# Attention encoder on one core: norm and table work moved between VectorE, ScalarE and GpSimd, inverse sums by transposed columns, value bank copied whole

## The chip, the cores and the metric

The kernel runs on one core of a Trainium2 chip. A core has a matrix engine (TensorE, PE), three engines for elementwise work (VectorE or DVE, ScalarE or ACT, GpSimd or POOL), a queue that issues transfers (SyncE, SP), a working memory (SBUF) and a small accumulator memory (PSUM), of which this kernel uses eight banks of 128 partitions by 512 fp32 columns. Each engine works through its own list of instructions in order and waits on semaphores for the others. The metric is the device time of one execution in microseconds.

## The reference

A layer over 2048 tokens of width 1024, one batch, all in fp32. The rows of x are normalised, scaled and shifted by functions of c, and projected by one matrix whose columns belong to three groups of heads. Each head's output is multiplied by a SiLU gate, all are concatenated, projected, gated, added to x, and normalised once more.

```python
h = rmsnorm(x, norm_g) * (1.0 + scale[:, None, :]) + shift[:, None, :]
z = h @ w_in                        # queries, keys, values, gates of A, B, C
a_out = mla_mixer(...)              # 6 heads, low-rank q and kv, block-causal
b_out = chunk_band_mixer(...)       # 5 heads, own chunk + 8 before, relative bias
c_out = forgetting_mixer(...)       # 5 heads, causal, cumulated forget logits
y = concatenate([a_out * silu(a_gate), b_out * silu(b_gate),
                 c_out * silu(c_gate)], axis=-1) @ w_out
x = x + gate[:, None, :] * y
return rmsnorm(x, final_g)
# each head: p = softmax(where(mask, s, NEG)); out = p @ v
```

## The kernel before

The tokens are done in two halves of 1024. In each half a projection stage (`stage_lv`) makes the latents, the values and the rotated queries and keys and stores them to DRAM. Then `attention` goes over 16 heads, two blocks of 512 queries each. To keep fp32 accuracy with the fast matmul type (fp32r), operands are split into a high part, rounded by an ACT copy, and a low part, the difference, and products are made of two or three matmuls.

A block of a head goes over tiles of 128 keys. For each tile PE makes scores in a PSUM bank `st` (three of these), ACT takes three exponentials of it (L753 the high part `ph`, L754 the sum's term `p`, L756 back into PSUM), DVE subtracts to get the low part `pl` (L762), POOL adds up `p` (L767), and PE multiplies `ph` and `pl` with the values into the one bank `pv` (L776, L777). At a block's end `end` (L779) copies `pv` in two pieces and POOL adds and gates them. Then come three steps at fixed distances of tiles, 1, 3 and 5: `sums` (L790) transposes the accumulated terms and reduces them, `rows` (L801) transposes the four inverse sums into rows and splits them, and `gate` (L808) spreads the rows over the partitions with a selecting matmul and multiplies. The maxima of the next block (`max_units`, L950 and L1036) and their transposition into a query row (`m_rows`) run beside this. All of these use two PSUM banks `mx`.

Projections of later heads, the gates, and for the second half the normalised and turned x (`h_units`, with bank `pj`) are cut into units and spread over a head's tiles by `Spread`; `mids` says which head carries what. In the first half the gate row is made in head 3, the row norms of the second half's x in head 7, its turned x in heads 14 and 15. In the second half `out_units` (output projection, residual, final norm) for eight of the 16 row tiles runs in heads 14 and 15, the other eight after them.

The Tile framework orders each engine's instructions from this program when it is built; the order is fixed then. It also keeps two engines from using one PSUM bank at the same time, so a bank passes from engine to engine with a wait.

Of the kernel before, what the change touches and what calls it, by code (L numbers as in the profile page):

```python
# [61 lines left out]
def kernel(ctx: ExitStack, tc: tile.TileContext, a: dict, out: bass.AP):  # L62
# [109 lines left out]
    def x_norm(xt, sq, r):  # L172
# [3 lines left out]
        V.tensor_scalar(vv, ss, 1.0 / D, EPS, op0=ALU.mult, op1=ALU.add)  # L176
        rsqrt(vv, 1, "xr", r)

    def h_units(hT, x_of, xn_of, tmp_of, ptag, norms=None):

        pairs = []
        for p2 in range(4):
            xns = []

            def norm(j, p2=p2, xns=xns):
# [7 lines left out]
                V.tensor_scalar(xn, xt, r, 0.0, op0=ALU.mult, op1=ALU.add)  # L193
                xns.append(xn)

            def turn(k, p2=p2, xns=xns, box={}):
# [10 lines left out]
                V.tensor_copy(hi, tmp)  # L207
# [153 lines left out]
    counters = {"m": 0, "r": 0, "p": 0}  # L361
# [74 lines left out]
    def latents(half, hT, wt, wt_pool, pool, lath, latl, h_pairs):  # L436
# [266 lines left out]
    def m_rows(pool, box, pm_of, dst, c8=None):  # L703
# [22 lines left out]
    def body_units(pool, kind, tb, par, scale, qk, V_of, sg_of, dst):  # L726
# [605 lines left out]
```

## Time and profile before

| | us |
|---|---|
| three runs | 1878.16, 1883.21, 1881.51 |
| median | 1881.51 |
| profiled execution | 1887.48 |
| its span, first to last instruction | 1885.4 |
| PE busy | 1743.9 |
| DVE busy | 1254.3 |
| ACT busy | 1181.6 |
| POOL busy | 985.7 |

Busy time is the time in which at least one instruction of the engine runs. Matmuls are pipelined: one of 512 columns is shown with about 0.40 us while the next starts about 0.23 us after it, so short waits of PE are hidden inside its busy time. The granted clock of PE over the whole run is 0.979.

The run falls into these parts: the start up to about 37 us, the first half's projections to about 250 us, its attention to about 755 us, the second half's projections to about 950 us, its attention to about 1790 us, and the last eight row tiles of the output.

### The profile page before, as it was taken

What the parts mean: (1) busy time and instruction counts of PE and PEld (TensorE: products, weight loads), DVE (VectorE), ACT (ScalarE), POOL (GpSimd) and SP (SyncE); (2) the same over time, 40 slices, a digit from 0 to 9 for tenths busy, and PEclk for the clock granted to TensorE, in tenths of its full rate; (3) what the DMA queues carried; (4) which work ended last, traced back from release to release, by engine and by line L of the source; (5) the groups of instructions that cost most, each with busy time, mean ns of one, the idle gap of its engine ahead of it and who ended that gap; (6) DMA issues with size and microseconds to landing.
All of it is one profiled execution on the core that took longest, in us unless ns stands there. A gap on an engine that the chain in (4) does not pass through costs nothing.

```text
span 1885.4 us, 28584 instructions
## 1 busy us (share of the span) xinstructions
PE 1743.9 (92%) x8899; PEld 1429.7 (76%) x8899; DVE 1254.3 (67%) x2905; ACT 1181.6 (63%) x2614; POOL 985.7 (52%) x902
## 2 busy tenths in 40 slices
PE   2999989998999997999999999999999989899897
PEld 2899877777777775999778777777777767677786
DVE  7663557777667679454466667787788887666543
ACT  2552357577667777342456677899899888555511
POOL 0320146555455557120145555677777788566744
PEclk9999999999999999999999999999999999999999
DMA  7524836335223232144933232222333344232243
GB/s 267 171 76 135 243 110 177 97 107 167 70 75 103 83 115 68 57 131 119 253 101 96 72 91 68 71 71 67 96 99 87 87 137 131 65 101 71 70 137 112
DMA packets 139996, 209.85 MB, mean 111 GB/s; under 512 B 18734, under 2 KB 72494, under 8 KB 139764
## 3 DMA queue, kind: packets, MB, share of 16 engines
q1 hardware_dynamic: 139844, 208.03, 37.2%
q8 instruction: 71, 1.16, 0.3%
q14 instruction: 81, 0.66, 0.1%
HBM read 154.05 MB, written 57.38 MB: 112 GB/s over the span
## 4 chain that ended last, share of the span: by engine, by line
PE 36%; DVE 5%; ACT 5%; issue 3%; POOL 1%; DMA 1%; DVEq 0%; POOLq 0%; ACTq 0%
PE pj L352 5%; PE pj L354 5%; PE pj L353 5%; PE pv L777 3%; PE pv L776 3%; PE st L996 2%; PE st L986 2%; PE mx L1044 2%; PE st L1054 2%; PE st L1055 1%; PE mx L963 1%; PE st L1056 1%; ACT st L756 1%; ACT p L754 1%; DVE pl L762 1%
## 5 line engine op out<-in xcount | busy, mean ns | idle before, releaser
L767 POOL TENSOR_TENSOR p<-p,p 128x512 f32<-128x512 f32 (+3 forms) x516 | 547.5, 1061 | 301.0 <-ACT p L754 267.3
L753 ACT ACTIVATE ph<-st 128x512 fp32r<-128x512 f32 (+1 forms) x580 | 297.7, 513 | 265.4 <-PE st L996 137.5
L762 DVE TENSOR_TENSOR pl<-st,ph 128x512 fp32r<-128x512 f32 (+1 forms) x580 | 333.3, 577 | 175.1 <-ACT st L756 161.2
L756 ACT ACTIVATE st<-st 128x512 f32<-128x512 f32 (+1 forms) x580 | 302.8, 522 | 0.0
L754 ACT ACTIVATE p<-st 128x512 f32<-128x512 f32 (+1 forms) x580 | 296.6, 511 | 0.0
L352 PE MATMUL pj<-hT,whi 128*128 128x512 f32 x544 | 225.3, 414 | 8.5 <-ACT q L920 8.4
L776 PE MATMUL pv<-ph,v 128*128 128x512 f32 (+1 forms) x580 | 215.1, 371 | 11.9 <-ACT ob L784 10.6
L777 PE MATMUL pv<-pl,v 128*128 128x512 f32 (+1 forms) x580 | 213.0, 368 | 12.0 <-DVE pl L762 11.4
L354 PE MATMUL pj<-hT,wlo 128*128 128x512 f32 x544 | 218.6, 402 | 0.0
L353 PE MATMUL pj<-hT,whi 128*128 128x512 f32 x544 | 218.5, 402 | 0.0
L1045 DVE TENSOR_REDUCE pm<-mx 128x1 f32<-128x512 f32 (+2 forms) x240 | 139.5, 603 | 22.6 <-PE mx L1044 20.6
L776 PEld LDWEIGHTS pv<-ph,v 128*128 128x128 f32 x580 | 111.6, 192 | 40.4 <-ACT ob L784 23.1
L777 PEld LDWEIGHTS pv<-pl,v 128*128 128x128 f32 x580 | 111.2, 192 | 38.9 <-DVE pl L762 22.0
L966 DVE TENSOR_REDUCE pm<-mx 128x1 f32<-128x512 f32 (+2 forms) x200 | 116.6, 605 | 30.6 <-PE mx L963 17.1
L996 PE MATMUL st<-q,k 128*128 128x512 f32 (+1 forms) x340 | 124.6, 370 | 0.9 <-DVE q L721 0.7
L785 POOL TENSOR_TENSOR oa<-oa,ob 64x512 f32<-64x512 f32 x64 | 83.7, 1308 | 76.3 <-ACT ob L784 49.8
L352 PEld LDWEIGHTS pj<-hT,whi 128*128 128x128 f32 x544 | 105.0, 193 | 23.8 <-ACT q L920 10.1
L986 PE MATMUL st<-q,k 128*128 128x512 f32 (+1 forms) x340 | 120.8, 356 | 1.2 <-DVE pl L762 0.9
L354 PEld LDWEIGHTS pj<-hT,wlo 128*128 128x128 f32 x544 | 104.4, 192 | 22.1
L353 PEld LDWEIGHTS pj<-hT,whi 128*128 128x128 f32 x544 | 104.8, 193 | 15.9
L1044 PE MATMUL mx<-k,q 128*128 128x512 f32 (+2 forms) x240 | 89.8, 394 | 20.6 <-DVE pm L1045 17.3
L354 PE MATMUL pj<-wo,ol 128*128 128x512 f32 x256 | 102.6, 401 | 2.1 <-POOL ol L1081 2.1
(398 smaller groups left out, 4245.2 us busy)
## 6 DMA issues: line engine op xcount, KB each, us to landing
wr<-in_w_in SPq DMA_DIRECT2D x54, 512.0 KB
wr<-in_x SPq DMA_DIRECT2D x34, 512.0 KB
v<-dva SPq DMA_DIRECT2D x36, 256.0 KB
q<-dqa SPq DMA_DIRECT2D x48, 192.0 KB
k<-dka SPq DMA_DIRECT2D x72, 128.0 KB
wa<-in_w_ada SPq DMA_DIRECT2D x16, 512.0 KB
do<-oo SPq DMA_DIRECT2D x64, 128.0 KB
wr<-do SPq DMA_DIRECT2D x128, 64.0 KB
```

Of the source, the lines that this page charges most:

```text
L352: T.matmul(dst, lhsT=lh, rhs=rh, start=i == 0, stop=False)
L353: T.matmul(dst, lhsT=lh, rhs=rl, start=False, stop=False)
L354: T.matmul(dst, lhsT=ll, rhs=rh, start=False, stop=i == n - 1)
L753: A.activation(ph[:, v0:v1], st[:, v0:v1], AF.Exp, scale=scale)
L754: A.activation(p32[:, v0:v1], st[:, v0:v1], AF.Exp, scale=scale)
L756: A.activation(st[:, v0:v1], st[:, v0:v1], AF.Exp, scale=scale)
L762: V.tensor_tensor(pl[:, c0:c1], st[:, c0:c1], ph[:, c0:c1].bitcast(F32), op=ALU.subtract)
L767: G.tensor_tensor(acc[:, c0:c1], acc[:, c0:c1], p32[:, c0:c1], op=ALU.add)
L776: T.matmul(pv[:, c0:c1], lhsT=vt, rhs=ph[:, c0:c1], start=n == 0, stop=False)
L777: T.matmul(pv[:, c0:c1], lhsT=vt, rhs=pl[:, c0:c1], start=False, stop=n == len(js) - 1)
L986: T.matmul(st[:, c0:c1], lhsT=k2[:, ks], rhs=q2[:, c0:c1], start=True, stop=False)
L996: T.matmul(st[:, c0:c1], lhsT=k1[:, ks], rhs=q1[:, c0:c1], start=False, stop=True)
```

## The change

Row norms: the steps on one number per row go from DVE to POOL. In `h_units` the product with the row norm goes from DVE to ACT, and the high part is made by DVE from PSUM instead of by a cast of ACT's copy. The inverse sums lose the step `rows`; `gate` transposes each column of four, broadcast to 128 columns, and runs three tiles after the block's end instead of five. `end` copies `pv` whole and takes the second copy from SBUF. The gate row is done in eight parts of two halves. The B heads' maxima no longer carry the constant c8 apart; it is taken out of the tables, which POOL scales. `evac` copies the key's high part to `k1` before it makes the low parts. For the eight row tiles of the output that lie in attention, the final norm's scaling is done by ACT and its product with `final_g` by POOL. The second half's turned x lies in heads 13, 14 and 15, and gate projection GA2 in head 12 instead of 13.

```diff
     def rsqrt(v, n, nm, r=None):
         G.tensor_tensor(y, v, mhalf[:, 0:n], op=ALU.pow)
-        V.tensor_tensor(t, y, y, op=ALU.mult)
-        V.tensor_tensor(t, t, v, op=ALU.mult)
-        V.tensor_scalar(t, t, -0.5, 1.5, op0=ALU.mult, op1=ALU.add)
-        V.tensor_tensor(r, y, t, op=ALU.mult)
+        G.tensor_tensor(t, y, y, op=ALU.mult)
+        G.tensor_tensor(t, t, v, op=ALU.mult)
+        G.tensor_scalar(t, t, -0.5, 1.5, op0=ALU.mult, op1=ALU.add)
+        G.tensor_tensor(r, y, t, op=ALU.mult)
...
     def h_units(hT, x_of, xn_of, tmp_of, ptag, norms=None):
-                V.tensor_scalar(xn, xt, r, 0.0, op0=ALU.mult, op1=ALU.add)
+                A.activation(xn, xt, AF.Copy, scale=r)
...
                 A.activation(tmp, tp, AF.Identity, scale=sc1[:, k:k + 1], bias=shf[:, k:k + 1])
-                V.tensor_copy(hi, tmp)
+                V.tensor_scalar(hi, tp, sc1[:, k:k + 1], shf[:, k:k + 1], op0=ALU.mult, op1=ALU.add)
...
     def gate_row(pool):
+        def part(k):
...
+            for c in range(2):
+                sl = slice(512 * c, 512 * c + 512)
+                if k == 0:
+                    V.tensor_scalar(acc[:, sl], wa[:, sl], cact[:, 0:1], 0.0, op0=ALU.mult, op1=ALU.add)
+                else:
+                    V.scalar_tensor_tensor(acc[:, sl], in0=wa[:, sl], scalar=cact[:, k:k + 1], in1=acc[:, sl], op0=ALU.mult, op1=ALU.add)
+        return [lambda k=k: part(k) for k in range(8)] + [lambda: gate_sum(pool, box["acc"])]
...
         def negate():
-            if c8 is None:
-                V.tensor_reduce(mp[:, 96:100], pm_of(), axis=AX.X, op=ALU.max, negate=True)
-            else:
-                m4 = pool.tile([128, 4], F32, tag="m4", name="m4")
-                V.reduce_max(m4, pm_of(), axis=AX.X)
-                V.tensor_scalar(mp[:, 96:100], m4, -1.0, c8(), op0=ALU.mult, op1=ALU.add)
+            V.tensor_reduce(mp[:, 96:100], pm_of(), axis=AX.X, op=ALU.max, negate=True)
...
         def end():
             pv = box["pv"]
+            ob = pool.tile([128, 512], F32, tag="oo", name="ob", bufs=2)
+            A.activation(ob, pv, AF.Copy)
             oa = pool.tile([128, 512], F32, tag="oa", name="oa", bufs=2)
-            A.activation(oa[o0:o1, :], pv[i0:i1, :], AF.Copy)
-            ob = pool.tile([128, 512], F32, tag="oo", name="ob", bufs=2)
-            A.activation(ob[o0:o1, :], pv[o0:o1, :], AF.Copy)
+            A.activation(oa[o0:o1, :], ob[i0:i1, :], AF.Copy)
...
-            rp = box["rp"] = rpads[counters["r"] % 2]
-            V.reciprocal(rp[:, 0:4], s4)
-        def rows():
-            rw = box["rw"] = rrows[counters["r"] % 2]
-            tp = pst("mx")
-            T.transpose(tp[:, 0:128], box["rp"], ident)
-            A.activation(rw[0:64, :], tp[0:64, 0:128], AF.Copy)
-            V.tensor_tensor(rw[64:128, :], tp[0:64, 0:128], rw[0:64, :].bitcast(F32), op=ALU.subtract)
+            rs = box["rs"] = pool.tile([128, 4], F32, tag="rs", name="rs")
+            V.reciprocal(rs, s4)
         def gate():
             rb = pst("mx")
             for t in range(4):
-                T.matmul(rb[:, 128 * t:128 * t + 128], lhsT=sel[:, t, :], rhs=box["rw"], start=True, stop=True)
+                T.transpose(rb[:, 128 * t:128 * t + 128], box["rs"][:, t:t + 1].to_broadcast([128, 128]), ident)
...
     def bias(self):
-            G.tensor_scalar(tb32[:, 0:384], tb32[:, 0:384], c8, 0.0, op0=ALU.add, op1=ALU.add)
-            V.tensor_scalar(tb32[:, 384:640], tb32[:, 384:640], 8.0, 0.0, op0=ALU.mult, op1=ALU.add)
-            V.tensor_scalar(te, te, 8.0, c8, op0=ALU.mult, op1=ALU.subtract)
+            G.tensor_scalar(tb32[:, 384:640], tb32[:, 384:640], 8.0, c8, op0=ALU.mult, op1=ALU.subtract)
+            G.tensor_scalar(te, te, 8.0, c8, op0=ALU.mult, op1=ALU.subtract)
-            evac_split(teh[:, 0:256], tel[:, 0:256], te)
+            A.activation(teh[:, 0:256], te, AF.Copy)
+            G.tensor_tensor(tel[:, 0:256], te, teh[:, 0:256].bitcast(F32), op=ALU.subtract)
...
     def evac(self, b, p):
             A.activation(q1[0:64, :], p[0:64, :], AF.Copy)
-            A.activation(k2[64:128, :], p[64:128, :], AF.Copy)
+            A.activation(k1[0:64, :], p[64:128, :], AF.Copy)
...
-            A.activation(k1[0:64, :], p[64:128, :], AF.Copy)
+            A.activation(k2[64:128, :], p[64:128, :], AF.Copy)
...
     def out_units(pool, wo, gate, fg, i):
             r = rsqrt(vv, 1, "xr")
+            if i < 8:
+                A.activation(xt, xt, AF.Copy, scale=r)
             for c in range(2):
-                V.scalar_tensor_tensor(xt[:, sl], in0=xt[:, sl], scalar=r, in1=fg[c], op0=ALU.mult, op1=ALU.mult)
+                if i < 8:
+                    G.tensor_tensor(xt[:, sl], xt[:, sl], fg[c], op=ALU.mult)
+                else:
+                    V.scalar_tensor_tensor(xt[:, sl], in0=xt[:, sl], scalar=r, in1=fg[c], op0=ALU.mult, op1=ALU.mult)
...
-                    tail.extend((clock[0] + d, u) for d, u in zip((1, 3, 5), t))
+                    tail.extend((clock[0] + d, u) for d, u in zip((1, 3), t))
...
-                mid = {1: "GA0", 2: "G1", 5: "GA1", 6: "G2", 9: "G3", 11: "G4", 13: "GA2"}
+                mid = {1: "GA0", 2: "G1", 5: "GA1", 6: "G2", 9: "G3", 11: "G4", 12: "GA2"}
...
-                mids[3] = mids.get(3, []) + [lambda: gate_row(pool)]
+                mids[3] = mids.get(3, []) + gate_row(pool)
...
-                mids[14] = h1[0] + h1[1]
-                mids[15] = h1[2] + h1[3]
+                h1 = sum(h1, [])
+                mids[13], mids[14], mids[15] = h1[:16], h1[16:32], h1[32:]
```

The order of instructions shows the moves at three places. The first is PE in the last heads of the first half, from the inverse sums of a block to their spreading; `rpad` holds the four inverse sums, `rrow` their rows, `c_ident` is the identity. Before:

```order
L804 MATMUL mx<-c_ident,rpad_253 128x128
L202 MATMUL pj<-c_ident,xn 128x128
L1044 MATMUL mx<-k_8124,q_8133 128x512
L202 MATMUL pj<-c_ident,xn 128x128 x3
L777 MATMUL pv<-pl,v 128x512
L1054 MATMUL st<-q_7821,k_7789 128x128
L1055 MATMUL st<-q_7821,k_7788 128x128
L1056 MATMUL st<-q_7822,k_7788 128x128
L776 MATMUL pv<-ph,v 128x384
L202 MATMUL pj<-c_ident,xn 128x128 x2
L720 MATMUL mx<-c_ident,mpad_251 128x128
L811 MATMUL mx<-rrow_256,sel 128x128 x3
```

After, from the sums of a block (L797) on; `rs` holds the inverse sums:

```order
L797 MATMUL mx<-c_ident,p_7880 128x128 x4
L779 MATMUL pv<-pl,v 128x256
L1050 MATMUL st<-q_7779,k_7733 128x512
L1051 MATMUL st<-q_7779,k_7732 128x512
L202 MATMUL pj<-c_ident,xn 128x128
L778 MATMUL pv<-ph,v 128x128
L1052 MATMUL st<-q_7780,k_7732 128x512 x2
L202 MATMUL pj<-c_ident,xn 128x128 x2
L806 MATMUL mx<-c_ident,rs 128x128 x4
L779 MATMUL pv<-pl,v 128x128
```

The transpose of `rpad` is gone, and the four transposes of `rs` follow the sums' own transposes after seven rows. The line numbers of the changed kernel are its own.

The second is DVE in the same heads, where the second half's x is made; `hT` is the turned x, `htmp` ACT's copy, `xn` the normalised rows. Before:

```order
L207 CAST hT<-htmp 128x256 x2
L721 TENSOR_TENSOR q_8171<-mx,sel 32x512
L796 TENSOR_REDUCE s_8651<-mx 128x4
L208 TENSOR_TENSOR hT<-htmp,hT 128x256
L799 RECIPROCAL rpad_254<-s_8651 128x4
L762 TENSOR_TENSOR pl<-st,ph 128x128
L207 CAST hT<-htmp 128x256 x2
L208 TENSOR_TENSOR hT<-htmp,hT 128x256
L762 TENSOR_TENSOR pl<-st,ph 128x512
L193 TENSOR_SCALAR xn<-wr,norms 128x1024 x2
L806 TENSOR_TENSOR rrow_255<-mx,rrow_255 64x128
```

After:

```order
L718 TENSOR_REDUCE mpad_252<-pm 128x4
L764 TENSOR_TENSOR pl<-st,ph 128x256
L207 TENSOR_SCALAR hT<-pj,sc_72,shf 128x256
L723 TENSOR_TENSOR q_7780<-mx,sel 32x512
L798 TENSOR_REDUCE s_8234<-mx 128x4
L207 TENSOR_SCALAR hT<-pj,sc_72,shf 128x256
L800 RECIPROCAL rs<-s_8234 128x4
L764 TENSOR_TENSOR pl<-st,ph 128x128
L208 TENSOR_TENSOR hT<-htmp,hT 128x256
L764 TENSOR_TENSOR pl<-st,ph 128x512
L207 TENSOR_SCALAR hT<-pj,sc_72,shf 128x256
L808 TENSOR_TENSOR oo<-mx,oa 64x512
```

The product `xn` and the difference `rrow` have left DVE, the casts of `htmp` have become scaled reads of the bank `pj`, and these lie farther apart.

The third is the final norm of the first row tile, before on DVE (`xvv` the mean square, `xrr` the inverse root, `wr` the row tile, `row` a row of `final_g`):

```order
L762 TENSOR_TENSOR pl<-st,ph 128x512
L1102 TENSOR_SCALAR xvv<-xss 128x1
L813 TENSOR_TENSOR oo<-mx,oa 64x512
L152 TENSOR_TENSOR xrt<-xry 128x1
L153 TENSOR_TENSOR xrt<-xrt,xvv 128x1
L154 TENSOR_SCALAR xrt<-xrt 128x1
L156 TENSOR_TENSOR xrr<-xry,xrt 128x1
L1106 SCALAR_TENSOR_TENSOR wr<-wr,xrr,row 128x512 x2
L1045 TENSOR_REDUCE pm<-mx 128x1
```

After, on POOL:

```order
L1092 TENSOR_TENSOR wr<-y,wr 128x512
L1098 TENSOR_SCALAR xvv<-xss 128x1
L150 TENSOR_TENSOR xry<-xvv,mhalf 128x1
L152 TENSOR_TENSOR xrt<-xry 128x1
L153 TENSOR_TENSOR xrt<-xrt,xvv 128x1
L154 TENSOR_SCALAR xrt<-xrt 128x1
L156 TENSOR_TENSOR xrr<-xry,xrt 128x1
L769 TENSOR_TENSOR p_18920<-p_18920,p_19226 128x512
L1105 TENSOR_TENSOR wr<-wr,row 128x512 x2
L1077 TENSOR_TENSOR ol<-wr,oh 128x1024
```

The whole chain and both products stand on POOL now, between additions of `p`; ACT's scaling between them stands on ACT.

## Rows read from the trace of the kernel before

**Rows 1.** The page, part 1: busy us, share of the span, instructions.

```profile
PE 1743.9 (92%) x8899; PEld 1429.7 (76%) x8899; DVE 1254.3 (67%) x2905; ACT 1181.6 (63%) x2614; POOL 985.7 (52%) x902
```

**Rows 2.** Stretches: busy us (xinstructions) by engine, then PE clock, DMA share, GB/s.

```profile
420.00:480.00 60.00, 51.67 (x245) 42.32 (x245) 41.20 (x105) 40.51 (x93) 32.43 (x33) 0.91 0.51 154
500.00:640.00 140.00, 136.12 (x710) 106.94 (x708) 89.67 (x182) 99.03 (x219) 75.11 (x65) 1.00 0.29 86
690.00:756.00 66.00, 52.06 (x267) 38.53 (x265) 60.30 (x126) 52.22 (x123) 45.21 (x47) 0.94 0.26 75
1200.00:1500.00 300.00, 297.19 (x1402) 226.22 (x1400) 238.54 (x432) 270.37 (x582) 224.38 (x186) 1.00 0.29 83
1600.00:1800.00 200.00, 182.05 (x798) 145.98 (x797) 122.46 (x203) 103.21 (x210) 123.52 (x98) 0.96 0.26 83
```

**Rows 3.** PE's waits over the run: us in total, times, longest us.

```profile
PE mx L242 <- DVE acc L240: 26.7, 2, 15.8
PE mx L1044 <- DVE pm L1045: 17.3, 11, 4.4
PE pv L777 <- DVE pl L762: 11.4, 9, 2.3
PE pv L776 <- ACT ob L784: 10.6, 20, 1.1
...
PE mx L720 <- DVE mpad L716: 5.2, 9, 1.0
...
PE mx L974 <- ACT k L919: 3.3, 7, 1.1
```

**Rows 4.** Timeline of DVE: start us, us, line, names, shapes, count.

```profile
706.86 3.50 DVE L193 TENSOR_SCALAR xn<-wr,norms 128x1024 f32<-128x1024 f32 x2
710.39 0.69 DVE L813 TENSOR_TENSOR oo<-mx,oa 64x512 f32<-64x512 f32 x1
...
1651.20 3.60 DVE L1106 SCALAR_TENSOR_TENSOR wr<-wr,xrr,row 128x512 f32<-128x512 f32 x2
...
1880.28 1.42 DVE L1106 SCALAR_TENSOR_TENSOR wr<-wr,xrr,row 128x512 f32<-128x512 f32 x2 [0.24 <-DVE xrr L156]
```

**Rows 5.** The second copy of pv (L784): ns min/median/max, and who waited.

```profile
L784 ACT ACTIVATE ob<-pv x64: 577/592/594, 271.7 to 1785.4; 64x512 f32<-64x512 f32 x64
...
  PEld pv L776: 23.1, 42
```

**Rows 6.** Inverse sums: four transposes in a row, weight loads, groups of PE.

```profile
270.66 0.60 PE L795 MATMUL mx<-c_ident,p 128*128 128x128 f32 x4
L795 PEld LDWEIGHTS mx<-c_ident,p x256: 137/141/224, 270.5 to 1782.9; 128*128 128x128 f32 x128
L811 PEld LDWEIGHTS mx<-rrow,sel x256: 186/192/337, 281.1 to 1788.4; 128*128 128x128 f32 x128
L811 PE MATMUL mx<-rrow,sel 128*128 128x128 f32 x256 | 40.6, 275 | 4.8 <-DVE rrow L806 3.7 <-DVE pm L1045 1.1
...
L804 PE MATMUL mx<-c_ident,rpad 128*128 128x128 f32 x64 | 17.7, 276 | 3.6 <-DVE rpad L799 2.1 <-DVE pm L1045 1.4
```

**Rows 7.** Groups by line and shape: busy us, mean ns of one, idle before.

```profile
L1106 DVE SCALAR_TENSOR_TENSOR wr<-wr,xrr,row 128x512 f32<-128x512 f32 x32 | 41.3, 1330 | 2.1 <-DVE xrr L156 1.4 <-DMA wr<-do 0.5
...
L207 DVE CAST hT<-htmp 128x256 fp32r<-128x256 f32 x64 | 21.8, 354 | 2.9 <-ACT htmp L204 2.6
...
L716 DVE TENSOR_SCALAR mpad<-m,c 128x4 fp32r<-128x4 f32 x20 | 7.9, 393 | 0.6
L1096 POOL TENSOR_TENSOR wr<-y,wr 128x512 f32<-128x512 f32 x32 | 41.3, 1291 | 37.1 <-DVE y L1095 33.9 <-issue 3.2
...
L903 POOL TENSOR_SCALAR tb<-tb,c 128x384 f32<-128x384 f32 x10 | 16.9, 1689 | 0.7
...
L901 POOL TENSOR_SCALAR c<-c 128x1 f32<-128x1 f32 x10 | 2.0, 204 | 48.2 <-DMA c<-in_rel_er 48.1
L753 ACT ACTIVATE ph<-st 128x512 fp32r<-128x512 f32 x343 | 206.6, 602 | 157.9 <-PE st L996 78.5 <-PE st L1056 66.4 <-issue 8.2
```

More of the change, by code (lines that the diff above doesn't have):

```diff
@@ L175, in x_norm @@
         A.activation(sq, xt, AF.Square, accum_out=ss)
-        V.tensor_scalar(vv, ss, 1.0 / D, EPS, op0=ALU.mult, op1=ALU.add)
+        G.tensor_scalar(vv, ss, 1.0 / D, EPS, op0=ALU.mult, op1=ALU.add)
         rsqrt(vv, 1, "xr", r)
@@ L264 @@
     mpads = [const.tile([128, 128], F32R, name=f"mpad{i}") for i in range(2)]
-    rpads = [const.tile([128, 128], F32, name=f"rpad{i}") for i in range(2)]
-    rrows = [const.tile([128, 128], F32R, name=f"rrow{i}") for i in range(2)]
-    for t in mpads + rpads:
+    for t in mpads:
         G.memset(t.bitcast(F32), 0.0)
@@ L312, in gate_row @@
     def gate_row(pool):
-        acc = pool.tile([128, D], F32, tag="xn", name="gacc", bufs=3)
-        for k in range(8):
+        box = {}
+        def part(k):
             wa = wr()
@@ L318, in gate_row, with gate_sum @@
             if k == 0:
-                V.tensor_scalar(acc, wa, cact[:, 0:1], 0.0, op0=ALU.mult, op1=ALU.add)
-            else:
-                V.scalar_tensor_tensor(acc, in0=wa, scalar=cact[:, k:k + 1], in1=acc, op0=ALU.mult, op1=ALU.add)
+                box["acc"] = pool.tile([128, D], F32, tag="xn", name="gacc", bufs=3)
+            acc = box["acc"]
+            for c in range(2):
[5 more added lines that the diff above has]
+        return [lambda k=k: part(k) for k in range(8)] + [lambda: gate_sum(pool, box["acc"])]
+    def gate_sum(pool, acc):
         bg = pool.tile([1, D], F32, tag="xn", name="bg", bufs=3)
@@ L359, in mm3 @@
             u()
-    counters = {"m": 0, "r": 0, "p": 0}
+    counters = {"m": 0, "p": 0}
     def any_bank():
@@ L450, in norm @@
             vv = col("lvv")
-            V.tensor_scalar(vv, ss[:, s:s + 1], 1.0 / n, EPS, op0=ALU.mult, op1=ALU.add)
+            G.tensor_scalar(vv, ss[:, s:s + 1], 1.0 / n, EPS, op0=ALU.mult, op1=ALU.add)
             r = rsqrt(vv, 1, "lr")
@@ L700, in values, with m_rows @@
         return made
-    def m_rows(pool, box, pm_of, dst, c8=None):
+    def m_rows(box, pm_of, dst):
         def negate():
@@ L814, in gate @@
             dma(out=dst[o0:o1, :], in_=oo[o0:o1, :])
-        return [(lambda n=n: scores(n), lambda n=n: parts(n), lambda n=n: values(n)) for n in range(len(js))], end, [sums, rows, gate]
+        return [(lambda n=n: scores(n), lambda n=n: parts(n), lambda n=n: values(n)) for n in range(len(js))], end, [sums, gate]
     QB, PB, LAG = 3, 3, 3
@@ L915, in evac @@
             A.activation(q1[0:64, :], p[0:64, :], AF.Copy)
+            A.activation(k1[0:64, :], p[64:128, :], AF.Copy)
+            V.tensor_tensor(q2[64:128, :], p[0:64, :], q1[0:64, :].bitcast(F32), op=ALU.subtract)
+            V.tensor_tensor(k2[0:64, :], p[64:128, :], k1[0:64, :].bitcast(F32), op=ALU.subtract)
             A.activation(k2[64:128, :], p[64:128, :], AF.Copy)
-            V.tensor_tensor(q2[64:128, :], p[0:64, :], q1[0:64, :].bitcast(F32), op=ALU.subtract)
-            V.tensor_tensor(k2[0:64, :], p[64:128, :], k2[64:128, :].bitcast(F32), op=ALU.subtract)
-            A.activation(k1[0:64, :], p[64:128, :], AF.Copy)
             A.activation(q2[0:64, :], p[0:64, :], AF.Copy)
@@ L978, in max_units @@
             return [lambda q=q, c=c: piece(q, c) for q in range(4) for c in range(nch)] + m_rows(
-                pool, box, lambda: box["pm"][:, :, 0:nch], lambda: self.qb[b][0], (lambda: self.c8) if kind == "B" else None)
+                box, lambda: box["pm"][:, :, 0:nch], lambda: self.qb[b][0])
         def qk(self, b, st, j, c0, c1):
@@ L1047, in max_units @@
             return [lambda q=q, c=c: piece(q, c) for q in range(4) for c in range(b + 1)] + m_rows(
-                pool, box, lambda: box["pm"][:, :, 0:b + 1], lambda: self.qb[b][1])
+                box, lambda: box["pm"][:, :, 0:b + 1], lambda: self.qb[b][1])
         def qk(self, b, st, j, c0, c1):
```

4 lines of the change are left out of this document (1 added, 3 removed).

## The prediction

> **What bounds the kernel now.** I read the page first, then stretches, then TensorE's (PE's) waits, then single lines. The page [rows 1]: PE is busy 92% of the span, VectorE (DVE) 67%, ScalarE (ACT) 63%, GpSimd (POOL) 52%. So some 140 us of PE idle are there to be won beside work that leaves PE, and 26.7 of them [rows 3] lie at the start, where the change does nothing. The stretches [rows 2] show how uneven the rest is. At 500 to 640 us PE is busy 136.1 of 140 (97%) at full clock. At 690 to 756 us, where the second half's x is normalised and turned, it is busy 52.1 of 66 while DVE is busy 60.3: DVE is the bound there. At 420 to 480 us (row norms of the second half's x) PE has 51.7 of 60, at 1600 to 1800 us (output projection with the final norm) 182.1 of 200. The granted clock of these three is 0.94, 0.91 and 0.96, so part of the time PE runs at 1.2 GHz of 2.4. At 1200 to 1500 us PE is at 99%, but ACT at 270.4 of 300 (90%) stands right behind it.
>
> PE waits most for DVE, through the maxima (17.3 us) and the low part of the exponentials (11.4), then for ACT's release of the one value bank pv (10.6) [rows 3].
>
> DVE is late because some of its instructions take far longer than their work [rows 4]. A pair of final-norm instructions (L1106) takes 1.42 us in the tail and 3.60 in attention; a pair of L193 takes 3.50. Both read and write SBUF only. L813, right behind that pair, reads PSUM and takes its 0.69. POOL works all this time in pieces of 1.3 us (L1096, [rows 7]). These long ones are what the change takes from DVE in attention.
>
> **The change part by part.** Sums stand against the profiled execution, 1887.5 us with a span of 1885.4. It lies 6.0 over the median of the runs, 1881.5; I take 6.0 off at the end.
>
> *A, value bank copied whole.* Two ACT copies of 0.59 us release pv now [rows 5], afterwards one of the full height. ACT's time goes by columns (L753, 128x512, 0.602, [rows 7]), so it costs the same 0.6; the second copy then reads SBUF. The next first value product may start up to 0.59 us earlier in each of 64 blocks. PE shows 10.6 us of it, its weight-load queue another 23.1 in 42 waits, partly under a matmul that still streams. Bounds 5 and 33.7; I take 12, near PE's own row.
>
> *B, inverse sums.* Per block one transpose (L804) goes, with ACT's copy and DVE's difference behind it; four selecting matmuls become four transposes of a broadcast column. A selecting matmul takes 275 ns and a transpose 276 [rows 6], so that swap is free if a broadcast column loads like a plain one, which no row shows. Four transposes take 0.60 us together, so one in a row costs (0.60 - 0.276)/3 = 0.11 us, times 64 = 7.0 of PE work gone. PE's waits in front of L804 (3.6) and L811 (4.8) belong to two hops that become one; I keep 1.4, which gives 7.0 more. B = 14, bounds 7 and 15.4.
>
> The Trainium skill, TensorE: Matmul & The Clock Gate, section Weight-path perf modes, says that fast weight load is on where there are 128 weights and their type is not FP32. By that the FP32 transposes would load slower than the fp32r selections that they replace. The loads here say the opposite, 141 ns for the FP32 ones against 192 [rows 6]. By the rule B would shrink, by the rows it stays.
>
> *C, maxima of the B heads.* L716, 20 times 0.39 us on DVE [rows 7], goes; the plain reduce in front of it then writes the result. PE waits 5.2 us for L716 [rows 3]. C = 4, bounds 0 and 5.2.
>
> *D, second half's x.* 40 units lie over three heads instead of two, and one gate projection moves a head earlier, the same PE work there. DVE hands eight L193 (1.75 us each in the pair shown) to ACT (8 x 1.2, two of L753's rows). L207, 0.354 now, reads PSUM: between that and L813's 0.69 for twice the columns, taken as 0.42, since it has half of them; 32 x 0.07 = 2 us more for DVE. PE idles 13.9 of 66. 1.8 is normal (2.8%, as at 500 to 640); A and B's 19 us over 64 blocks, 0.3 each, account for some 1.5; 10.6 remain, and 2 from the clock. Against this stands a new alternation: ACT's and DVE's scaled copies read the same bank, and in the built program each waits for the other, so ACT pauses in 16 banks, 0.2 to 0.3 us each beyond what exponentials between them hide: minus 4. D = 8, bounds -5 and 12.6.
>
> *E, row norms at 420 to 480 us.* The small DVE steps go to POOL, where the chain's power already is; a step of that size takes 0.20 us there (L901, [rows 7]), and the hops between the engines go. PE idles 8.3; 1.7 is normal, 1.5 in A and B. E = 5, bounds 0 and 8.
>
> *F, final norm in attention.* 16 of the 32 L1106 leave DVE: 16 x 1.33 = 21 us of 200 [rows 7]. POOL gets 16 products of 1.29 (L1096's size) and eight chains of five 0.2 us steps, some 29 us: from 123.5 to about 152 of 200 [rows 2], still under PE. ACT gets 8 x 1.2 and waits for the chain. PE idles 17.9; 5.6 normal, 1.5 in A and B, 10.8 left, of which I drop 3 for ACT's waits. F = 8, bounds -3 and 12.
>
> The Trainium skill, GPSIMD Engine Reference, section Engine selection, gives elementwise work to VectorE, since a two-input operation is about twice as slow on GpSimd. In the tail the rows agree (0.71, half of the pair, against 1.29). In attention they don't: L1106 takes 1.33 in the mean. By the rule F would be a loss, by the rows it costs nothing.
>
> *G, k before its low part.* The maxima wait 3.3 us for ACT's k copy, which now runs two places earlier: 2, bounds 0 and 3.3.
>
> *At about nothing.* Gate row in parts: the same columns on DVE. Norms during the projections: the same chain, off PE's path but for its first links. Bias tables: POOL loses L903 (1.69 us) and gains two scalings of 256 columns (1.13 each at L903's rate) and a difference, so ACT's teh comes some 2 us later in 10 heads; the exponentials placed around it hide that, else it is up to 20 us.
>
> Sum 12 + 14 + 4 + 8 + 5 + 8 + 2 = 53. A and B's waits, 19 us, lie for about half in blocks like those of 1200 to 1500 us, where ACT at 90% is late next: minus 9.5. That leaves 43.5: 1844.0 on the profile's scale, 1838 against the median. All lower bounds: 5 + 7 + 0 - 5 + 0 - 3 + 0 = 4; all upper: 33.7 + 15.4 + 5.2 + 12.6 + 8 + 12 + 3.3 = 90. So 1791 to 1878.
>
> **Rivals.**
> 1. *The next wait takes over.* ACT's three exponentials per tile (1.8 us, three of L753) bind wherever DVE did. For it: ACT's 90%. Against it: 52 of 66 and 103 of 200 in the two worst stretches [rows 2]. Then B's work and a third of A, D and F remain, 7 + 9 = 16, or 1866.
> 2. *The broadcast column loads slowly.* Place: the 256 loads that follow on L811's, in PE's order. Nearest slow row: the longest load of L811, 337 ns against 141 [rows 6]. Price 256 x 0.196 = 50, time 1888, slower. It decides from 43.5/256 = 0.17 us per load. Against it: plain loads of either type hide under the matmul before.
> 3. *ACT is held by POOL and DVE* (teh ten times 2 us, the bank alternation 16 times 0.5 more): 28 us, half of which reaches PE; 1852.
> 4. *The low clock goes too.* If the stalls of the three stretches go as a whole and A comes near its upper bound, the gain is 80 and the time 1802.
>
> **How the numbers follow.** The forecast, 1838, has its own range 1815 to 1861 and a chance of 0.56; rival 1 0.16, rival 2 0.08, rival 3 0.09, rival 4 0.11. A measurement of this kernel tells 0.3% (5.6 us) from no change. Faster takes the forecast, rivals 3 and 4 and two thirds of rival 1: 0.87. Same, 0.05, is the rest of rival 1. Slower, 0.08, is rival 2. The range, 1798 to 1876, leaves out rival 2 and the far end of rival 4.
>
> **What would show it.** Right: in attention no SBUF-only DVE instruction of over 1 us is left but the weight splits and the gate row; the second half's h takes some 100 us with PE over 93%; four broadcast transposes stay at 0.6 us; PE's waits for ob halve; POOL is near 75% at 1600 to 1800 us. Wrong: broadcast loads well over 0.2 us, ACT idling for POOL's te or DVE's hT, or PE as idle as now with ACT as the releaser in place of DVE.

## The result, and the profile after

The changed kernel takes 1864.33 us in the median of 4 runs (1863.08 to 1866.33), the kernel before 1879.84 (4 runs): a ratio of 0.9919, 95% interval 0.9896 to 0.9942. That is 15.5 us faster; the forecast was 43.5. The profiled execution took 1863.1 us with a span of 1861.1. That is 1.2 us under its median, while the profile of before lies 7.6 us over its own, so the two profiles stand 24.3 us apart and show some 9 us more than the change gained.

The page's part 1, of after (compare [rows 1]):

```profile
PE 1714.6 (92%) x8835; PEld 1415.7 (76%) x8835; DVE 1132.8 (61%) x2447; ACT 1195.3 (64%) x2574; POOL 1071.9 (58%) x1256
```

DVE lost 121.5 us of busy time and POOL took over 86, as intended; PE's busy time fell by 29.3 us, and its idle time went from 141.5 to 146.5.

The stretches, of after (columns as in [rows 2]; the fifth line, the second half's heads A0 to A3, before the output projection's matmuls begin to dominate, is new):

```profile
420.00:480.00 60.00, 58.57 (x304) 48.02 (x301) 38.79 (x80) 50.24 (x113) 46.48 (x80) 1.00 0.51 162
500.00:640.00 140.00, 138.48 (x719) 108.94 (x719) 85.57 (x162) 103.61 (x220) 72.52 (x63) 1.00 0.29 87
690.00:756.00 66.00, 48.17 (x240) 36.74 (x239) 51.47 (x94) 49.30 (x104) 37.75 (x41) 0.92 0.25 72
1200.00:1500.00 300.00, 289.12 (x1368) 222.99 (x1366) 231.19 (x415) 267.28 (x564) 224.16 (x185) 0.99 0.28 81
1430.00:1600.00 170.00, 152.00 (x677) 117.88 (x676) 129.14 (x223) 142.01 (x298) 129.62 (x104) 0.94 0.39 111
1600.00:1800.00 200.00, 190.03 (x864) 154.16 (x863) 80.67 (x136) 108.14 (x204) 154.90 (x169) 1.00 0.29 92
```

The fifth line, of before:

```profile
1430.00:1600.00 170.00, 160.35 (x719) 123.69 (x718) 135.60 (x239) 152.28 (x323) 141.25 (x111) 0.97 0.42 116
```

The row norms (first line, 51.67 before) and the final norm (last line, 182.05 before) gained what was asked, and more. At 1200 to 1500 us PE is busy 8 us less than before, and at 1430 to 1600 us 152 of 170, where it had 160.35.

These stretches lie at fixed times, and what runs in them moves when the kernel gets ahead. The third line is not comparable: the last block of the first half now ends at 741.0 us instead of 753.6 (start of the copy of `pv`), and from 750 us on PE is busy all the time with the second half's projections. The starts of these copies (L784) tell better where time goes. At the block that before ends at 618.3 us the changed kernel is ahead by 17.5 us, at the second half's first (974.8) by 9.7: some 8 us go where x is made and just behind. At the block of 1429.1 us it is ahead by 22.0, at that of 1605.5 by 10.7, at the last one (1785.4) by 25.6: another 11 us go in the heads A0 to A3.

PE's waits, of after (columns as in [rows 3]):

```profile
PE mx L242 <- DVE acc L240: 26.7, 2, 15.7
PE pv L779 <- DVE pl L764: 22.5, 18, 4.9
PE pj L359 <- ACT q L916: 14.0, 2, 7.4
PE pv L778 <- ACT ob L784: 9.8, 21, 1.5
PE mx L1040 <- DVE oo L808: 8.9, 5, 2.4
PE mx L1040 <- DVE pm L1041: 7.4, 6, 2.3
PE st L202 <- DVE hT L207: 4.6, 4, 2.2
```

The maxima's wait for DVE more than halved (17.3 to 7.4), but pl's doubled (11.4 to 22.5), a bank held by the gate product (oo, L808) has come in with 8.9, and the wait for the copy of the value bank (ob) is as long as it was (10.6 and 9.8).

DVE's waits name what holds it: the gate product (oo) waits for oa, the block's output after POOL's addition (L787) and gating (L788). Of after, then of before:

```profile
DVE oo L808 <- POOL oa L788: 32.6, 13, 5.9
```

```profile
DVE oo L813 <- POOL oa L786: 2.4, 1, 2.4
```

One case of it, in the chain that ended last (start us, us, what; head A3, of after):

```profile
1567.26 0.52 ACT ob L784
1567.77 0.39 ACT ph L755
1568.16 0.88 issue
1569.04 1.29 POOL oa L787
...
1570.40 1.29 POOL p L769
...
1571.78 1.28 POOL oa L788
1573.05 0.02 issue
1573.08 0.70 DVE oo L808
1573.78 0.04 issue
1573.83 0.50 PE mx L1040
1574.33 0.43 PE pj L359
```

ACT and PE there (start us, us, of after):

```profile
1567.07 0.71 ACT L784 ACTIVATE ob<-pv 128x512 f32<-128x512 f32 x1
1567.54 0.71 ACT L755 ACTIVATE ph<-st 128x512 fp32r<-128x512 f32 x1
1568.28 0.63 ACT L786 ACTIVATE oa<-ob 64x512 f32<-64x512 f32 x1
```

```profile
1571.85 0.40 PE L778 MATMUL pv<-ph,v 128*128 128x512 f32 x1
1573.83 0.50 PE L1040 MATMUL mx<-k,q 128*128 128x512 f32 x1 [1.58 <-DVE oo L808]
```

The bank is copied at once (ob), but the second copy, now a reader of ob, starts behind an exponential (L755), and POOL puts an addition of `p` (L769) between its two steps. oa is ready at 1573.05, 6.0 us after the first copy's start. DVE takes its instructions in order, so the maximum and pl behind the gate product stand still; PE waits 1.58 us for the bank that the gate product reads. Stretches around it (columns as above):

```profile
1570.00:1574.00 4.00, 2.42 (x12) 1.46 (x11) 1.58 (x3) 4.00 (x10) 3.76 (x4) 1.00 0.23 72
1574.00:1578.00 4.00, 4.00 (x12) 2.95 (x13) 3.12 (x6) 1.09 (x3) 2.96 (x3) 0.57 0.35 72
```

PE is busy 2.42 of 4 us, and in the 4 after that its granted clock is 0.57, so most of them at 1.2 GHz.

### The profile page after: what moved, and what is told of

It reads as the page before. It is cut to its first block, busy times and chain, and to the rows that moved or that the text cites. A ratio compares the mean times of both kernels' runs of the same rounds, so it can differ in the third digit from the quotient of the medians.

```text
span 1861.1 us, 28271 instructions
## 1 busy us (share of the span) xinstructions
PE 1714.6 (92%) x8835; PEld 1415.7 (76%) x8835; DVE 1132.8 (61%) x2447; ACT 1195.3 (64%) x2574; POOL 1071.9 (58%) x1256
## 4 chain that ended last, share of the span: by engine, by line
PE 41%; ACT 7%; POOL 4%; issue 3%; DVE 3%; DMA 1%; SPq 0%; ACTq 0%; DVEq 0%; POOLq 0%
PE pj L359 5%; PE pj L360 5%; PE pj L361 5%; PE pv L778 3%; PE pv L779 3%; PE st L992 2%; PE st L982 2%; ACT st L758 1%; PE mx L1040 1%; PE mx L959 1%; ACT ph L755 1%; ACT p L756 1%; PE st L1051 1%; PE st L1052 1%; POOL p L769 1%
## 5 line engine op out<-in xcount | busy, mean ns | idle before, releaser
L769 POOL TENSOR_TENSOR p<-p,p 128x512 f32<-128x512 f32 (+3 forms) x516 | 539.7, 1046 | 248.8 <-ACT p L756 206.5
L755 ACT ACTIVATE ph<-st 128x512 fp32r<-128x512 f32 (+1 forms) x580 | 299.3, 516 | 226.8 <-PE st L992 121.6
L779 PE MATMUL pv<-pl,v 128*128 128x512 f32 (+1 forms) x580 | 213.9, 369 | 22.8 <-DVE pl L764 22.5
L787 POOL TENSOR_TENSOR oa<-oa,ob 64x512 f32<-64x512 f32 x64 | 82.7, 1292 | 82.8 <-ACT oa L786 49.7
L1040 PE MATMUL mx<-k,q 128*128 128x512 f32 (+2 forms) x240 | 85.5, 387 | 17.3 <-DVE oo L808 8.9
L359 PE MATMUL pj<-wo,oh 128*128 128x512 f32 x256 | 101.1, 395 | 0.0
```

Of the source, the lines that this page charges most:

```text
L359: T.matmul(dst, lhsT=lh, rhs=rh, start=i == 0, stop=False)
L755: A.activation(ph[:, v0:v1], st[:, v0:v1], AF.Exp, scale=scale)
L769: G.tensor_tensor(acc[:, c0:c1], acc[:, c0:c1], p32[:, c0:c1], op=ALU.add)
L779: T.matmul(pv[:, c0:c1], lhsT=vt, rhs=pl[:, c0:c1], start=False, stop=n == len(js) - 1)
```

## The experiments

All times are medians of 4 to 12 runs; the kernel before had medians of 1879.7 to 1882.5 in the five groups of runs, so across groups differences under some 4 us are not told. Names stand for edits of the changed kernel.

**gate5**

```diff
-                    tail.extend((clock[0] + d, u) for d, u in zip((1, 3), t))
+                    tail.extend((clock[0] + d, u) for d, u in zip((1, 5), t))
```

> The changed kernel with the gate product issued 5 tiles behind the end of its block, as its last step was before, instead of 3; all else as changed. Theory: in the changed profile VectorE's gate product (L808) waits 32.6 us in 13 waits for GpSimd's product oa (L788), which comes 5.6 to 6 us after the value bank's copy begins; VectorE works in order, so the maxima and pl behind it come late to TensorE. With 5 tiles that wait falls under 5 us and the kernel gains 8 to 15 us on the changed one (1849 to 1856). Rival: the gain was lost elsewhere (the exponentials on ScalarE, second half's x, the start): the wait falls as well, but the time stays within 4 us (1860 to 1868).

Measured 1858.7, ratio 0.9872 (0.9847 to 0.9898). 5.7 us faster, between the theory's range and the rival's; DVE's wait for oa fell only to 25.7 us in 9. The direction is the theory's, and 5 tiles are not enough to tell.

**cast**

```diff
-                V.tensor_scalar(hi, tp, sc1[:, k:k + 1], shf[:, k:k + 1], op0=ALU.mult, op1=ALU.add)
+                V.tensor_copy(hi, tmp)
```

> The changed kernel with L207 as before: VectorE makes the fp32r half of hT from ScalarE's htmp in SBUF instead of reading the PSUM bank once more. Theory 1 (ScalarE and VectorE take turns at the bank and hT is released to TensorE later): the start's 5.6 us, the second half's 4.9 us lost while x is spread, and some of the 2.9 us at the second projections come back, so 5 to 12 us faster than the changed kernel (1852 to 1859). Theory 2 (the late gate product is the loss, the bank is not): within 4 us of the changed kernel (1860 to 1868).

Measured 1859.0 (0.9873, 0.9851 to 0.9896): 5.4 us faster, at the edge of theory 1 and outside theory 2. The trace has the place of theory 1: PE is busy 64.5 of the first 100 us (59.8 in the changed kernel), and DVE's wait for oa stays (32.2 us).

**spread**

```diff
-                mid = {1: "GA0", 2: "G1", 5: "GA1", 6: "G2", 9: "G3", 11: "G4", 12: "GA2"}
+                mid = {1: "GA0", 2: "G1", 5: "GA1", 6: "G2", 9: "G3", 11: "G4", 13: "GA2"}
...
-                h1 = sum(h1, [])
-                mids[13], mids[14], mids[15] = h1[:16], h1[16:32], h1[32:]
+                mids[14] = h1[0] + h1[1]
+                mids[15] = h1[2] + h1[3]
```

> The changed kernel with second half's x put back into heads 14 and 15 (20 units each, the gate row's loads at head 13) instead of 13 to 15. The prediction gave this part 8 us: then it is 8 us slower than the changed kernel (1872). The changed trace lost 4.9 us in that stretch: if the spreading does it, this one is 3 to 6 us faster (1858 to 1861). If the bank's second reader does it (L207), the time hardly changes (within 3 us).

Measured 1859.1 (0.9873, 0.9850 to 0.9896): 5.3 us faster. Spreading x, with the gate projection GA2 moved for it, is a loss, not a gain of 8; the two were not tried apart.

**end2**

```diff
-            A.activation(ob, pv, AF.Copy)
-            oa = pool.tile([128, 512], F32, tag="oa", name="oa", bufs=2)
-            A.activation(oa[o0:o1, :], ob[i0:i1, :], AF.Copy)
+            oa = pool.tile([128, 512], F32, tag="oa", name="oa", bufs=2)
+            A.activation(oa[o0:o1, :], pv[i0:i1, :], AF.Copy)
+            ob = pool.tile([128, 512], F32, tag="oo", name="ob", bufs=2)
+            A.activation(ob[o0:o1, :], pv[o0:o1, :], AF.Copy)
```

> The changed kernel with the value bank copied in two halves from PSUM again (both by ScalarE, oa first), the rest as changed. The prediction gave this part 12 us (5 to 33.7): then 12 us slower than the changed kernel (1876). Against it stands that TensorE's wait for the bank's copies is as long after as before (10.6 and 9.8 us in MATMUL, 23.1 and 22.6 in weight loads) and that oa now starts from SBUF later, which VectorE's gate product waits for: if that cancels, this kernel is within 4 us of the changed one or up to 6 us faster.

Measured 1854.0 (0.9844, 0.9818 to 0.9869): 10.3 us faster, more than either view had. PE waits longer for the bank (17.3 us against 9.8), yet DVE's wait for oa falls to 20.1 us. The stretch that lost, of end2:

```profile
1430.00:1600.00 170.00, 160.18 (x723) 125.41 (x722) 133.62 (x232) 146.11 (x304) 136.83 (x108) 0.97 0.39 113
```

PE is back at 160.2 of 170 there (152.0 in the changed kernel, 160.35 before). With the gate 3 tiles behind, the whole copy costs.

**sums3** is end2 with the inverse sums as before, in steps of 1, 3 and 5 tiles (the edit in part):

```diff
-                T.transpose(rb[:, 128 * t:128 * t + 128], box["rs"][:, t:t + 1].to_broadcast([128, 128]), ident)
+                T.matmul(rb[:, 128 * t:128 * t + 128], lhsT=sel[:, t, :], rhs=box["rw"], start=True, stop=True)
...
-        ... [sums, gate]
+        ... [sums, rows, gate]
```

> Bank copied in two halves and the inverse sums as before: one padded transpose, its split, four selecting matmuls, in three steps 1, 3 and 5 tiles behind; the rest as changed. Against the kernel with the two halves alone (1854.0). Theory as in the prediction (B is worth 14: 64 transposes of 0.11 us and two hops made one): 1868. Rival 1: PE's 7 us of work are the whole of it, the hop was hidden: 1861. Rival 2: TensorE's work is given back because something else ends last there and the longer way (gate 5 tiles behind) also spares VectorE its remaining wait for oa (20.1 us in 10): 1850 to 1857.

Measured 1876.1 (0.9986, 0.9969 to 1.0002): 22.1 us over end2, more than any view had, though the gate product has its 5 tiles back here. The group that the change removed, of sums3 (busy us, mean ns of one, idle before), and one of its transposes between matmuls of 512 columns (start us, us):

```profile
L808 PE MATMUL mx<-c_ident,rpad 128*128 128x128 f32 x64 | 17.9, 279 | 4.7 <-DVE pm L1051 2.4 <-DVE rpad L803 2.2
```

```profile
1223.59 0.39 PE L362 MATMUL pj<-hT,whi 128*128 128x512 f32 x1
1223.82 0.40 PE L363 MATMUL pj<-hT,wlo 128*128 128x512 f32 x1
1224.06 0.27 PE L808 MATMUL mx<-c_ident,rpad 128*128 128x128 f32 x1
1224.08 0.48 PE L361 MATMUL pj<-hT,whi 128*128 128x512 f32 x1
1224.40 0.39 PE L362 MATMUL pj<-hT,whi 128*128 128x512 f32 x1
```

It would be easy to add 17.9 and 4.7 and call that the 22.1. The starts say otherwise: from the lone transpose to the second matmul behind it pass 0.34 us, where one matmul takes 0.23. So this lone transpose costs PE 0.11 us, as one in a row of four, and its shown 0.27 overlaps what follows; of the 27 between undisturbed matmuls of this size, 24 cost that. At this price the 64 are worth the 7 us that the prediction gave. The other 15 us are no work of PE's own that these rows show. In the profiles 14.6 us of the difference are there by the copy of the fourteenth block of 64 (480.6 us in sums3, 466.0 in end2); which waits make them is open.

**final**

```diff
-            if i < 8:
+            if False:
                 A.activation(xt, xt, AF.Copy, scale=r)
...
-                if i < 8:
+                if False:
                     G.tensor_tensor(xt[:, sl], xt[:, sl], fg[c], op=ALU.mult)
```

> The changed kernel with the final norm's scaling in attention as before (one VectorE instruction per half row, fed by the norm's steps on GpSimd as now); the rest as changed. The prediction gave this part 8 (bounds -3 and 12): then 1872. In the changed trace the last two heads (A4, A5) gained 13 us on before, so if that is all this part's, 1877. If the gain there comes from the whole of the change (VectorE's other work, the sums), up to 4 slower only (1864 to 1868).

Measured 1878.9 (0.9987, 0.9974 to 1.0000): 14.6 slower. Stretch of final:

```profile
1600.00:1800.00 200.00, 182.05 (x799) 147.73 (x798) 110.07 (x150) 98.01 (x194) 133.75 (x142) 0.95 0.25 78
```

PE is busy 182.05 here, as before the change [rows 2], at a clock of 0.95: what the change gained in this stretch, it gained by moving these instructions off DVE.

**best1** joins end2, cast and spread; **best2** adds gate5.

> The changed kernel with three parts undone together: bank copied in two halves, L207 from SBUF, second half's x in heads 14 and 15. If the three gains (10.3, 5.4 and 5.3 us) have separate places, they add up to 21: 1843. If the last two are one loss (VectorE and ScalarE in the second half's x and the start) or overlap with the first in the same waits, 1847 to 1851. If two of them are only the spread of single programs, 1852 to 1855.

> The same three undone, and the gate product 5 tiles behind. If VectorE's remaining wait for oa (20.1 us in 10 with the halves) still costs, 2 to 6 us under the kernel before this one. If oa was the copy's fault alone, the gate step costs nothing more: within 3 us of it, or slower by the tail's two more tiles.

Measured 1844.8 (0.9809, 0.9786 to 0.9833) and 1839.9 (0.9787, 0.9764 to 0.9809). The three nearly add up, and the later gate gives 4.9 more even with two halves, though DVE's wait for oa stays (20.7 us in 7 and 20.6 in 6), so this wait is not the whole of what the distance does.

**whole7** is cast and spread with the bank copied whole, as changed, and offsets (1, 7).

> The bank copied whole as changed, L207 and second half's x as before, the gate product 7 tiles behind. In the changed trace the bank's second copy stands behind an exponential and GpSimd puts an addition between its two products, so oa is ready some 6 us after the copy; TensorE waits less for the bank (9.8 us against 17.3 with two halves). Theory (the wait of VectorE for oa is all that the whole copy loses): 7 tiles take the wait away, and with the shorter wait for the bank this is equal to or up to 7 us faster than the halves with the gate 5 behind (1839.9): 1833 to 1840. Rival (the copies' place among the exponentials costs by itself): 1844 to 1850, though the product no longer waits.

Measured 1828.0 (0.9714, 0.9693 to 0.9735): 5 us under the theory's range, and 16 under the rival's, which is out. Waits of PE and DVE, of whole7:

```profile
PE pv L779 <- DVE pl L764: 8.4, 10, 1.8
...
PE pv L778 <- ACT ob L784: 5.3, 11, 1.6
```

```profile
DVE oo L808 <- POOL oa L788: 11.7, 3, 5.9
```

pl's wait is 8.4 us (22.5), the bank's 5.3 (16.7 in best2). Of DVE's 11.7 us for oa half is one wait of 5.9, which the changed kernel shows too.

**b2bias**, on best2:

```diff
-            G.tensor_scalar(te, te, 8.0, c8, op0=ALU.mult, op1=ALU.subtract)
+            V.tensor_scalar(te, te, 8.0, c8, op0=ALU.mult, op1=ALU.subtract)
...
-            A.activation(teh[:, 0:256], te, AF.Copy)
-            G.tensor_tensor(tel[:, 0:256], te, teh[:, 0:256].bitcast(F32), op=ALU.subtract)
+            evac_split(teh[:, 0:256], tel[:, 0:256], te)
```

> The kernel with the halves, L207 from SBUF, second half's x in two heads and the gate 5 behind (1839.9), with the bias tables' scalings and the low half of teh on VectorE instead of GpSimd (13.1 us of ScalarE's waits for te in 3, and 14.0 us of TensorE's for q in 2, in the changed trace). Theory: ScalarE's wait for te holds q's copy at the start of each half, so 3 to 6 us faster: 1834 to 1837. Rival: the projections behind hide it, and VectorE gets 20 instructions more among the maxima: within 3 us, 1837 to 1843.

Measured 1837.7 (0.9766, 0.9749 to 0.9784): 2.2 us, in the rival's range and too little to tell.

**b2norm**, on best2: `G.tensor_...` to `V.tensor_...` in the mean square and Newton lines.

> The kernel of 1839.9 us with the norms' small steps (mean square, Newton) on VectorE again, everywhere. The prediction gave this 5 us (bounds 0 and 8) at the row norms of 420 to 480 us: then 1845. The changed trace gained 12.3 us there: if the steps alone did it, 1852, and more where the final norm's chain crosses engines again. If the gain came from the sums and the gate row, within 3 us: 1837 to 1843.

Measured 1849.7 (0.9830, 0.9812 to 0.9848): 9.8 us slower. At 420 to 480 us, of b2norm:

```profile
420.00:480.00 60.00, 53.02 (x259) 43.47 (x258) 43.33 (x106) 42.07 (x94) 33.08 (x35) 0.94 0.48 152
```

```profile
420.00:480.00 60.00, 58.43 (x301) 48.33 (x301) 39.77 (x84) 50.31 (x112) 47.64 (x81) 1.00 0.49 153
```

PE falls back to 53.0 of 60 from the 58.4 of best2 (second line; 51.67 before), so the steps' place makes that stretch.

**b2evac**, on best2: k's copy behind its low part again.

> The kernel of 1839.9 us with k copied after its low part again (the order before). The prediction gave this 2 us (bounds 0 and 3.3): then 1842. Within what can be told (3 us) is the likeliest; faster by over 3 us would show that the low part of k, which the scores need first, was held up by the new order.

Measured 1838.7 (0.9773, 0.9755 to 0.9791): no difference that can be told.

**gate7** is the changed kernel with (1, 7) for (1, 3), nothing else; **halves7** is best2 with (1, 7).

> The changed kernel with one number altered: the gate product 7 tiles behind instead of 3; x spread over three heads and L207 from PSUM stay as changed. If the early gate product is the one fault that hides the whole copy's gain (11.9 us between best2 and whole7), and the x parts cost what they cost beside it (5.4 and 5.3), this is 1828 + 10 = 1838, the time that the prediction gave. If the x parts' loss came through the same wait, 1830 to 1834. If the early gate has no part in it, 1858 as with 5 tiles.

> The kernel with two halves, L207 from SBUF, second half's x in two heads (best2, 1839.9), gate product 7 tiles behind instead of 5. whole7 differs from best2 in two things, the whole copy and 2 tiles more. If the whole copy is worth what the prediction said once nothing waits for oa (12), this stays within 3 us of 1839.9. If the 2 tiles did it, it comes to 1828 to 1832.

Measured 1842.4 (0.9811, 0.9792 to 0.9831), 4 us over the 1838 expected, and 1834.9 (0.9766, 0.9752 to 0.9781). One number gives 22 us. Stretch and wait of gate7:

```profile
1200.00:1500.00 300.00, 298.36 (x1419) 231.85 (x1418) 238.29 (x427) 276.19 (x585) 231.92 (x192) 1.00 0.29 85
```

```profile
DVE oo L808 <- POOL oa L788: 11.7, 3, 6.0
```

PE is busy 298.4 of 300 (289.1 in the changed kernel) with ACT at 276.2. DVE's wait for oa falls from 32.6 to 11.7 us, and PE's waits for pl, ob and the bank of oo (L1040) from 22.5, 9.8 and 8.9 to 10.3, 5.7 and 0.2. The place fits too: gate7 is ahead of the changed kernel by 7.8 us at the copy of the block that the latter has at 1407.1 us, and by 20.5 at that of 1594.8, so most of the gain is where the changed kernel fell back. The distance also moves PE's four transposes and the use of the bank `mx`; what these do by themselves was not tried.

Between halves7 and whole7 only the copy differs: with the gate late it is worth 7.0 us, not 12, and PE waits 5.3 us for the bank where halves7 has 12.5. Two more tiles behind best2 are worth 4.9; halves7 missed its 3 us for that reason.

**whole7b** is whole7 with b2bias's edit, **whole9** has (1, 9), **maxc** is whole7b with the B heads' maxima in two DVE steps, **whole7c** is whole7b with b2evac's edit.

> whole7 (1828.0) with the bias tables' scalings and teh's low half on VectorE: with best2 that gave 2.2 us. The same gain again: 1824 to 1827. If the whole copy's order uses VectorE's idle time, 1828 or slower.

> whole7 with the gate product 9 tiles behind. In whole7 VectorE still waits 11.7 us in 3 for oa, the longest 5.9 at the very end where nothing else is left. If the waits in attention are gone, 9 tiles give nothing: 1826 to 1830; the maxima's gate banks then only hold mx longer, 1830 to 1835 if that matters.

> whole7b (1823.2) with the maxima of the B heads in two VectorE steps again (a plain reduce, then a negating step of four columns, 20 times 0.39 us). The prediction gave this part 4 us (bounds 0 and 5.2): 1827. If the step is hidden behind other maxima: 1821 to 1825.

> whole7b (1823.2) with k copied after its low part, as before. The prediction gave the new order 2 us: 1825. In the kernel with two halves the old order was 1.2 us faster, less than can be told: 1822 to 1824 if the order does nothing.

Measured: whole7b 1823.2 (0.9706, 0.9692 to 0.9721), the fastest beside whole7c, 56 us under the kernel before; whole9 1836.9 (0.9775, 0.9759 to 0.9790), 9 us slower than 7 tiles and not foreseen; why was not tried. maxc 1827.9 (0.9704, 0.9686 to 0.9722) and whole7c 1825.3 (0.9694, 0.9676 to 0.9713) are 4.7 and 2.1 us over whole7b by their times, but the kernel before was 2.7 slower in their group, and by the ratios they are no slower: neither part can be told from nothing.

## Why the prediction was wrong

| term | forecast (bounds) | gain measured, us, by times (by ratios) | from |
|---|---|---|---|
| A, whole copy | 12 (5 to 33.7) | at 3 tiles -10.3 (-14.1), at 7 +7.0 (+9.8) | end2; halves7 and whole7 |
| B, inverse sums | 14 (7 to 15.4) | 22.1 (26.7) | sums3 and end2 |
| C, B heads' maxima | 4 (0 to 5.2) | none told: 4.7 (-0.4) | maxc |
| D, x and L207 | 8 (-5 to 12.6) | -14.4 (-18.2) | gate7 and whole7 |
| E, norms' steps | 5 (0 to 8) | 9.8 (8.1) | b2norm and best2 |
| F, final norm | 8 (-3 to 12) | 14.6 (12.8) | final |
| G, k first | 2 (0 to 3.3) | none told: -1.2 (-2.6), 2.1 (-2.3) | b2evac, whole7c |
| bias tables | 0 | -2.2 (-3.9), -4.7 (-1.5) | b2bias, whole7b |

Most of these compare kernels of different groups, so each has a second figure, the difference of the two ratios times 1880; the two lie up to some 5 us apart. The parts were also taken out of different kernels, so that the sum is a check and no proof. With A at 7 tiles and bias at -4.7 these add up to 34.4; gate7 gains 37.3 on the kernel before. The early gate product takes 22 of it: 15.5 is left. By the ratios it is 37.7 against 35.5.

**The step that failed first** is B's "two hops become one; I keep 1.4", with A's "it costs the same 0.6; the second copy then reads SBUF". The change brings the gate product from 5 tiles behind to 3 and puts oa one link further back, and no term priced that product's wait for oa; the working listed what PE waits for, not what the moved instruction itself needs. An estimate from the case above: three tiles are nine exponentials, there some 0.49 us from start to start, about 4.4 us; oa's chain there takes 1.97 us from the first copy to POOL and two POOL steps of 1.29, over 4.5 even without the addition. The runs put a number on it: the distance alone is worth 22 us (gate7). The step also misplaced A: the early release was real (PE's wait for the bank 12.5 to 5.3 us at 7 tiles), and at 3 tiles what it gave was paid back by DVE.

**The second step** is D. L207 was taken as 0.42 us; with two per-partition scalars from PSUM it takes 0.534 to 0.538. DVE then waits for ACT's copy of the same bank, and PE's transposes in turn for hT (4.6 us in 4 cases at the start), which the term had only as ACT's pauses. Rows of after, with their idle time before:

```profile
L207 DVE TENSOR_SCALAR hT<-pj,sc,shf 128x256 fp32r<-128x256 f32 x32 | 16.9, 534 | 1.6 <-ACT htmp L204 1.3
L207 DVE TENSOR_SCALAR hT<-st,sc,shf 128x256 fp32r<-128x256 f32 x32 | 16.3, 538 | 14.1 <-ACT htmp L204 14.0
```

The 64 of them cost 33.2 us against 21.8 [rows 7], and the same edit sits in the start, which the prediction said the change leaves alone: PE is busy 59.8 of the first 100 us in the changed kernel and 64.4 in whole7. That L207 and the spreading each cost about 5 alone and 14.4 together at 7 tiles is measured. The copies of `pv` place it: whole7 is ahead of gate7 by 5.3 us at the first block (270.4 and 275.7 us), so the start has cost that much, and by 11.5 at the first block of the second half (951.4 and 962.9), so about 6 more went between them, where x is made. Which wait makes these 6 stays open, and so does what is over 11.5.

**Too small** were B, E and F. In B the work was priced right and the waits were not; which ones is open. In F the 16 products were taken at 1.33 us, the mean of all 32; the 16 in attention keep DVE busy 25.7 us of the profile before, not 21. In both E and F the clock went along: with the instructions back on DVE their stretches have a granted clock of 0.94 (b2norm) and 0.95 (final), with them moved off it 1.00.

**Right** were the direction; the sign of F, which by the rule of the Trainium skill (GPSIMD Engine Reference, section Engine selection) that the prediction cites would have been a loss, while final measured a gain of 14.6 us; POOL's load at 1600 to 1800 us (154.9 of 200); and that broadcast columns load like plain ones, which ends rival 2. Their loads take 136 ns in the median and 230 at most, where the plain ones of before took 141 [rows 6]. Loads and matmuls of after:

```profile
L806 PEld LDWEIGHTS mx<-c_ident,rs x256: 132/136/230, 282.2 to 1763.3; 128*128 128x128 f32 x128
L806 PE MATMUL mx<-c_ident,rs 128*128 128x128 f32 x256 | 40.0, 278 | 4.7 <-DVE rs L800 2.4 <-DVE pm L1041 2.1
```

Two of the prediction's own signs said that it was wrong: PE's waits for ob did not halve, and where x is made (640 to 740 us) PE is busy 80.0 of 100 us and not over 93%.

Rival 1 gave 1866, close to the time, but that is luck: ACT was not the next limit, since gate7 runs PE at 99% with ACT busier than before (276.2 against 270.4 [rows 2]). So the 9.5 us taken off for ACT were not due either. Rival 3's alternation at the bank is part of D, by cast. Rival 4's low clock did go in E and F.

## What to carry to other kernels

When a change moves an instruction forward in an in-order engine, price its own operands first: how long after the common starting point is each ready, and what stands behind it in the queue. A copy that frees a buffer early may still make its other reader late, so the consumer's distance belongs to the copy; here the best distance tried was 7 tiles, with 3, 5 and 9 all worse. What a short matmul costs is read from the starts around it, not from its busy time, even when a sum with the busy time comes out.

## What was not expected of the hardware

- ACT's copy from SBUF took 0.630 us for 64x512, no less than the 0.603 us of 128x512 from PSUM.
- A DVE read of PSUM with two per-partition scalars took 0.534 us for 256 columns; the 512-column product from PSUM without them (L808) took 0.687.
- One stall of PE, 1.6 us, was followed by 4 us at a granted clock of 0.57.
- A lone transpose of 128 columns, shown with 0.27 us, put off the matmuls behind it by 0.11 us.
